# Splitting a float32 product into rounded halves: input halves side by side in one matmul, and expert outputs summed token by feature

## The chip, the cores and the metric

One core of a Trainium2 chip runs the whole program. The time is device time in microseconds from the start to the end of the program, and less is better. The engines are named as in the profile: PE is TensorE (matmuls), PEld its weight loads, DVE VectorE, ACT ScalarE, POOL GpSimd, SP SyncE.

## What is computed

Two blocks on a stream of 256 tokens with 2048 features, in float32. The first block has an RWKV-7 time mix and a sparse attention side by side, then a feed-forward of 16384 experts of which each token picks 8 x 16; the second an HGRN2 layer and a forgetting attention. Cut to the parts that the change touches:

```python
def _rmsnorm(x, g): return x / sqrt(mean(x * x) + eps) * g

xn = _rmsnorm(h, norm_mix_g)
p_rw, q, c_kv, iq, ik, iw, gates = split(xn @ w_in)        # 2048 -> 9320
h = h + (sigmoid(ga) * (y_a @ w_branch_rwkv) + sigmoid(gb) * (y_b @ w_branch_dsa)) @ w_out
hn = _rmsnorm(h, norm_ffn_g)
q = hn @ w_peer_query                                       # keys of the picks
act = gelu(einsum('nd,nhkd->nhk', hn, expert_u[eid]))       # eid: the picked experts
h = h + einsum('nhk,nhkd->nd', gate * act, expert_v[eid])
x = x + hgrn2(norm(x) @ a_w_in) @ a_w_out                   # second block
x = x + forgetting_attention(norm(x) @ b_w_in, k, v, F) @ b_w_out
```

## The kernel before

**Layout.** The stream and nearly all activations lie as [feature, token]: 16 chunks (KD) of 128 partitions by 256 tokens (T). Weights come from memory as tiles of [128, 1024] float32, 512 KB each, on SyncE's queue (`raw`, L348, three slots).

**Float32 by halves.** The matmuls take operands rounded to a shorter float (float32r), so each operand is split exactly into a high and a low part: `half_split` (L354) makes `whi` by a ScalarE copy (L359) and `wlo` by a subtraction on VectorE (L360; for half of the query weights on GpSimd), 512 columns at a time, five slots each. `split` (L396) does the same with activations. A product is then high x high + high x low + low x high.

**Projections.** `proj_steps` (L372) makes one tile of 128 output features: for each of 16 chunks it loads 128 weight columns as the stationary operand and streams 256 tokens, three times (L383 to L385), all into one accumulator `pm` of [128, 256] (two slots, each a bank):

```python
nc.tensor.matmul(ps, hi[:, s], xh, start=(c == 0), stop=False)
nc.tensor.matmul(ps, hi[:, s], xl, start=False, stop=False)
nc.tensor.matmul(ps, lo[:, s], xh, start=False, stop=(c == n - 1))
```

There are 330 such projections of 16 chunks, and 32 of 8 chunks (the two branches' output, `w_br`). `evac` (L594) reads the accumulator on VectorE and multiplies it by the norm's scale R; 274 projections end there, 8 (the attention's queries) in `pair_inputs` (L586), and 48 (`w_out`, `a_w_out`, `b_w_out`) in an addition to the stream.

**Projections with tokens on the partitions.** `tok_steps` (L1331, L1340 to L1342) does it the other way round: 128 tokens of the activations are stationary and 512 weight columns stream, three matmuls for each of two token tiles. The value, key and query blocks of the second block use it.

**Experts.** All 16384 experts are computed densely, in 128 tiles of 128; `ups` (L1094) makes the activations, one projection per tile, up to six groups of 8 tiles ahead. Beside the first of them the queries are scored and the top 16 picked (`select`, L1113: the score matmuls at L1121 read `dq`, what `evac` made of the query projection), then one-hot products make the gate matrix (`onehots`, L1212). `weigh` (L1245) multiplies a group's activations by their gates and splits them (`cs`), and `down` (L1256) sums the group's outputs: for each of 16 feature chunks d, 8 expert tiles x 3 matmuls of 256 columns (L1264 to L1266), then the sum is added to the stream h[d] on VectorE (L1267). 16 groups make 2048 matmuls on each of the three lines.

**Order.** Work is written as generators whose steps `interleave` mixes; the tile scheduler lays out each engine's instructions at compile time by that order and by its own estimate of when each is ready. On the chip every engine runs its list in order. In the HGRN stage `heads` (L1415) is a chain that passes between ACT, DVE, POOL (L1452, L1504) and PE (L1475) while the next projections run beside it.

Of the kernel before, what the change touches and what calls it, by code (L numbers as in the profile page):

```python
# [73 lines left out]
def _consts():  # L74
# [8 lines left out]
    # [128, 16]: column 2j+h of a window that starts at 14-2j is the indicator of half h  # L83
# [20 lines left out]
    # [s, t] inside a tile, t of the second halves of the blocks of 2 * 2**l: pairs that part at level l  # L104
# [4 lines left out]
    # [t, s]: -1e30 above the diagonal  # L109
# [31 lines left out]
def pack(i):  # L141
    """Every input as the kernel loads it: tiles in the order of their use, each contiguous."""
# [98 lines left out]
def interleave(*streams):  # L241
    """(generator, number of its steps): one step of whichever is least far"""
# [16 lines left out]
def after(n, do, steps):  # L259
    """the steps, and do() after n of them"""  # L260
# [5 lines left out]
def lagged(steps, lag):  # L266
    """the generators side by side, each lag steps behind the one before"""
# [13 lines left out]
class Kern:  # L281
    # names of tiles that share slots
    GROUP = {}
    for _g, _n in dict(
        tmp="xc bias sq rs pd th b bx eb ei kk rk st y yo mix relu Rc ck score ld k4",
        mv="rz vz dq",
# [7 lines left out]
    def __init__(self, tc, a, out, es, dbg=None):  # L294
# [7 lines left out]
        self.open("all", ah=17, al=17, nacc=4, nsq=3)  # L302
# [7 lines left out]
    def open(self, name, **slots):  # L310
        """a pool with so many slots for each group of tiles; its memory waits for nothing but the tiles there"""
# [16 lines left out]
    # ---- small helpers  # L328
# [5 lines left out]
    def pm(self, w=T):  # L334
        return self.pp.tile([P, w], F32, name="pm", tag="pm", bufs=2)
# [12 lines left out]
    def raw(self, src):  # L348
        """1024 or 512 columns of weights"""
# [4 lines left out]
    def half_split(self, raw, i, eng=None):  # L354
        """exact (hi, lo) of half i of raw"""
# [12 lines left out]
    def proj(self, src, act, eng=None):  # L368
        """src [128, K]: one tile of 128 output features; act: (hi, lo) of the inputs, per k chunk [128, T]."""
        return finish(self.proj_steps(src, act, eng))  # L370

    def proj_steps(self, src, act, eng=None, ps=None, step=8):  # L372
# [3 lines left out]
        for c in range(n):  # L376
            xh, xl = act[c]
# [18 lines left out]
    def split(self, x, g=None, tag=None, out=None):  # L396
        """exact (hi, lo) of x or x*g, g a column"""
        nc = self.nc
        hi, lo = out or (self.t1(tag or "ah", dt=F32R), self.t1(tag or "al", dt=F32R))
# [6 lines left out]
        return hi, lo  # L406

# [1417 lines left out]
```

## Time and profile before

| | |
|---|---|
| median of 3 runs | 3615.51 us (3613.62 to 3616.02) |
| span of the profiled execution | 3613.2 us |
| TensorE busy | 3563.3 us, 99%, 29630 matmuls |
| VectorE, ScalarE, GpSimd busy | 71%, 52%, 12% |
| memory read | 595 MB, 171 GB/s over the span |

The profiled execution lies 2.3 us below the median of the runs. Busy time of TensorE counts overlapping matmuls as one, so it doesn't tell how close they follow each other; the order in time does. The program's stages by time: mixer to 590 us, branches and output to 870, peer queries to 1110, one-hots to 1340, experts to 2540, HGRN to 3050, forgetting attention to the end.

### The profile page before, as it was taken

The page shows a single profiled execution, that of the slowest core. Times are in us where ns is not written, and L with a number is a line of the kernel's source. Part 1 is how long each engine was busy: PE and PEld are TensorE (multiplying, and loading weights), DVE is VectorE, ACT ScalarE, POOL GpSimd, SP SyncE. Part 2 cuts the span into 40 slices and gives each one's busy share as a digit, 9 for nine tenths or more (in the row PEclk, how much of TensorE's full clock was granted, in tenths as well). Part 3 has the DMA queues.
Part 4 walks back from the last instruction along what each step waited for, and adds up shares of the span by engine and source line. Part 5 has one row for each costly group of instructions (what it writes and reads, how often), then busy time and mean ns, then how long its engine had stood idle before and what let it go on. Part 6 is the DMA issues. An engine that isn't in the chain of part 4 may idle for free.

```text
span 3613.2 us, 76495 instructions
## 1 busy us (share of the span) xinstructions
PE 3563.3 (99%) x29630; PEld 3398.9 (94%) x29630; DVE 2582.2 (71%) x5410; ACT 1874.0 (52%) x3695; POOL 436.8 (12%) x488
## 2 busy tenths in 40 slices
PE   8999999999999999999999999999999999999999
PEld 7888889999999999999999999999899999888899
DVE  6767766666999987666666666667768887657775
ACT  5443444445445664444444444445556665566653
POOL 1121110001234420000000000000013340000010
PEclk9999999999999999999999999999999999999999
DMA  7422225555455677666666665555644436665445
GB/s 224 157 95 77 73 82 158 182 186 194 161 167 176 217 243 245 195 194 195 197 193 195 196 194 184 183 183 181 193 150 139 135 123 185 192 194 169 127 146 179
DMA packets 204636, 619.26 MB, mean 171 GB/s; under 512 B 19520, under 2 KB 60848, under 8 KB 202096
## 3 DMA queue, kind: packets, MB, share of 16 engines
q1 hardware_dynamic: 197616, 604.06, 52.7%
q10 hardware_dynamic: 5888, 8.20, 0.7%
q8 instruction: 234, 3.83, 0.4%
q0 software_dynamic: 768, 2.10, 0.2%
q14 instruction: 130, 1.06, 0.1%
HBM read 595.32 MB, written 21.06 MB: 171 GB/s over the span
## 4 chain that ended last, share of the span: by engine, by line
PE 84%; issue 5%; DVE 5%; DMA 4%; ACT 1%; POOL 1%; SPq 0%; DVEq 0%; ACTq 0%; POOLq 0%
PE pm L383 16%; PE pm L385 15%; PE pm L384 15%; PE pm L1264 6%; PE pm L1266 6%; PE pm L1265 6%; PE pa L758 3%; DVE wlo L360 2%; PE pa L1228 2%; DMA wraw<-w_pq 1%; PE pa L1475 1%; PE pa L1340 1%; PE pa L1341 1%; PE pa L1342 1%; PE pm L1342 1%
## 5 line engine op out<-in xcount | busy, mean ns | idle before, releaser
L360 DVE TENSOR_TENSOR wlo<-wraw,whi 128x512 fp32r<-128x512 f32 x2114 | 1522.3, 725 | 737.4 <-ACT whi L359 690.5
L359 ACT ACTIVATE whi<-wraw 128x512 fp32r<-128x512 f32 x2152 | 1343.9, 631 | 1335.7 <-PE pm L384 706.4
L383 PE MATMUL pm<-ah,whi 128*128 128x256 f32 x4384 | 1279.0, 292 | 1.0 <-ACT nacc L438 1.0
L385 PE MATMUL pm<-ah,wlo 128*128 128x256 f32 x4384 | 1248.4, 285 | 10.4 <-DVE wlo L360 8.5
L384 PE MATMUL pm<-al,whi 128*128 128x256 f32 x4384 | 1245.4, 284 | 0.0
L383 PEld LDWEIGHTS pm<-ah,whi 128*128 128x128 f32 x4384 | 843.5, 192 | 26.0 <-issue 15.7
L385 PEld LDWEIGHTS pm<-ah,wlo 128*128 128x128 f32 x4384 | 843.2, 192 | 16.6 <-DVE wlo L360 12.0
L384 PEld LDWEIGHTS pm<-al,whi 128*128 128x128 f32 x4384 | 844.3, 193 | 0.9
L1264 PE MATMUL pm<-cs,whi 128*128 128x256 f32 x2048 | 581.2, 284 | 1.0 <-ACT whi L359 0.8
L1266 PE MATMUL pm<-cs,wlo 128*128 128x256 f32 x2048 | 580.9, 284 | 0.0
L1265 PE MATMUL pm<-cs,whi 128*128 128x256 f32 x2048 | 580.9, 284 | 0.0
L1264 PEld LDWEIGHTS pm<-cs,whi 128*128 128x128 f32 x2048 | 394.0, 192 | 1.5 <-ACT whi L359 1.5
L1265 PEld LDWEIGHTS pm<-cs,whi 128*128 128x128 f32 x2048 | 394.1, 192 | 0.0
L1266 PEld LDWEIGHTS pm<-cs,wlo 128*128 128x128 f32 x2048 | 394.1, 192 | 0.0
L442 POOL TENSOR_TENSOR nacc<-nacc,nsq 128x256 f32<-128x256 f32 x35 | 29.0, 836 | 1396.6 <-ACT nsq L441 1375.8
L384 PE MATMUL pm<-keep,whi 128*128 128x256 f32 x640 | 181.3, 283 | 0.0
L1267 DVE TENSOR_TENSOR h<-pm,h 128x256 f32<-128x256 f32 x256 | 108.3, 423 | 40.0 <-PE pm L1266 37.1
L384 PEld LDWEIGHTS pm<-keep,whi 128*128 128x128 f32 x640 | 123.2, 193 | 0.0
L1099 ACT ACTIVATE ga<-kk 128x256 f32<-128x256 f32 x128 | 52.9, 413 | 114.4 <-DVE kk L595 114.4
L385 PE MATMUL pm<-keep,wlo 128*128 128x256 f32 x384 | 108.0, 281 | 0.0
L383 PE MATMUL pm<-keep,whi 128*128 128x256 f32 x384 | 108.0, 281 | 0.0
L1340 PE MATMUL pa<-whi,ah 128*128 128x512 f32 x256 | 102.5, 400 | 0.0
(414 smaller groups left out, 5050.5 us busy)
## 6 DMA issues: line engine op xcount, KB each, us to landing
wraw<-peer_u SPq DMA_DIRECT2D x256, 512.0 KB, 3.8
wraw<-peer_v SPq DMA_DIRECT2D x256, 512.0 KB, 3.5
wraw<-w_in SPq DMA_DIRECT2D x136, 512.0 KB, 3.8
wraw<-a_w_in SPq DMA_DIRECT2D x96, 512.0 KB, 3.8
wraw<-w_br SPq DMA_DIRECT2D x32, 512.0 KB, 3.5
wraw<-w_out SPq DMA_DIRECT2D x32, 512.0 KB, 4.3
wraw<-w_pq SPq DMA_DIRECT2D x32, 512.0 KB, 4.3
gates<-gst SPq DMA_DIRECT2D x16, 1024.0 KB, 5.5
```

The lines of the kernel that those rows point to most:

```text
L359: nc.scalar.activation(hi, x, AF.Copy)
L360: (eng or nc.vector).tensor_tensor(lo, x, hi.bitcast(F32), op=OP.subtract)
L383: nc.tensor.matmul(ps, hi[:, s], xh, start=(c == 0), stop=False)
L384: nc.tensor.matmul(ps, hi[:, s], xl, start=False, stop=False)
L385: nc.tensor.matmul(ps, lo[:, s], xh, start=False, stop=(c == n - 1))
L758: nc.tensor.matmul(ps[h, c], lhs[h, c], rhs[h, c], start=True, stop=True)
L1228: nc.tensor.matmul(p[:, v], one[:, v], two[:, v], start=True, stop=True)
L1264: nc.tensor.matmul(ps, hi[:, s], ch, start=(e == 0), stop=False)
L1265: nc.tensor.matmul(ps, hi[:, s], cl, start=False, stop=False)
L1266: nc.tensor.matmul(ps, lo[:, s], ch, start=False, stop=(e == GE - 1))
L1267: nc.vector.tensor_tensor(h[d], ps, h[d], op=OP.add)
L1340: nc.tensor.matmul(ps[tt], xh[:, t], hi, start=(c == 0), stop=False)
```

## The change

**Projections.** The high and low half of an activation now lie side by side in one tile [128, 2, 256] (`pair`), and the accumulator `pm` is 512 columns wide. High weights stream both halves at once, 512 columns; low weights stream the high half, 256 columns, into the first half of the accumulator. At the end the two halves of the accumulator are added: a ScalarE copy of the second half (`pb`, which shares the three slots of `nsq`), then a VectorE addition. The branch projections keep the old form. `evac` multiplies by R on GpSimd afterwards; the three residual additions use `add`, with two VectorE additions.

**Expert outputs.** `down` uses `tok_steps`: the weighted activations are stationary, 512 columns of expert weights stream. Sums stay as [token, feature] in eight SBUF tiles `ys` over all 16 groups and are transposed back and added to h during and after the last group (`back`). The expert weights are laid out anew in memory for it.

**Pools.** Slots are renamed and resized to fit (peer: `keepR`, `tmp` 8 to 7; experts: `cs` 24 to 23, `yt` 8; fox: `keep` 48 to 8 and `keep2` 21 tiles of twice the size).

```diff
-    v = f("peer_v")[0].reshape(P, NG, GE, KD, P)
-    a["peer_v"] = np.ascontiguousarray(v.transpose(1, 3, 0, 2, 4)).reshape(NG, KD, P, GE * P)
+    v = f("peer_v")[0].reshape(P, NG, GE // 2, 2, 4, 512)
+    a["peer_v"] = np.ascontiguousarray(v.transpose(1, 4, 2, 0, 3, 5)).reshape(NG, 4, GE // 2, P, 1024)
...
-    def pm(self, w=T):
+    def pm(self, w=512):
...
     def proj_steps(self, src, act, eng=None, ps=None, step=8):
...
-            xh, xl = act[c]
+            x = act[c]
...
-            nc.tensor.matmul(ps, hi[:, s], xh, start=(c == 0), stop=False)
-            nc.tensor.matmul(ps, hi[:, s], xl, start=False, stop=False)
-            nc.tensor.matmul(ps, lo[:, s], xh, start=False, stop=(c == n - 1))
+            if isinstance(x, tuple):
+                xh, xl = x
+                nc.tensor.matmul(ps[:, :T], hi[:, s], xh, start=(c == 0), stop=False)
+                nc.tensor.matmul(ps[:, :T], hi[:, s], xl, start=False, stop=False)
+                nc.tensor.matmul(ps[:, :T], lo[:, s], xh, start=False, stop=(c == n - 1))
+            elif c < n - 1:
+                nc.tensor.matmul(ps, hi[:, s], x.rearrange("p a t -> p (a t)"), start=(c == 0), stop=False)
+                nc.tensor.matmul(ps[:, :T], lo[:, s], x[:, 0], start=False, stop=False)
+            else:
+                nc.tensor.matmul(ps[:, :T], lo[:, s], x[:, 0], start=False, stop=False)
+                nc.tensor.matmul(ps, hi[:, s], x.rearrange("p a t -> p (a t)"), start=False, stop=True)
...
+    def join(self, ps, out):
+        b = self.t1("pb")
+        self.nc.scalar.activation(b, ps[:, T:], AF.Copy)
+        self.nc.vector.tensor_tensor(out, ps[:, :T], b, op=OP.add)
+
+    def add(self, x, ps, out=None):
+        b = self.t1("pb")
+        self.nc.scalar.activation(b, ps[:, T:], AF.Copy)
+        self.nc.vector.tensor_tensor(x, ps[:, :T], x, op=OP.add)
+        self.nc.vector.tensor_tensor(x if out is None else out, x, b, op=OP.add)
...
+    def pair(self, x, g=None, tag="ah", out=None):
+        t = self.t1(tag, (P, 2, T), F32R) if out is None else out
+        self.split(x, g, out=(t[:, 0], t[:, 1]))
+        return t
...
-        self.nc.vector.scalar_tensor_tensor(q, ps, 0.125, self.R, op0=OP.mult, op1=OP.mult)
+        self.join(ps, q)
+        self.nc.vector.scalar_tensor_tensor(q, q, 0.125, self.R, op0=OP.mult, op1=OP.mult)
...
     def evac(self, ps, out):
-        self.nc.vector.tensor_tensor(out, ps, self.R, op=OP.mult)
+        self.join(ps, out)
+        self.nc.gpsimd.tensor_tensor(out, out, self.R, op=OP.mult)
...
-        self.open("experts", gt=2, cs=24)
+        self.close()
+        self.open("experts", gt=2, cs=23, yt=8)
+        ys = [[self.t1("yt", (P, 512)) for _ in range(4)] for _ in range(2)]
...
+        def back(b):
+            for d in range(4 * b, 4 * b + 4):
+                ps = self.pa(T)
+                s = slice(d % 4 * P, d % 4 * P + P)
+                for tt in range(2):
+                    nc.tensor.transpose(ps[:, tt * P : tt * P + P], ys[tt][b][:, s], self.cst("ident"))
+                yield
+                nc.vector.tensor_tensor(h[d], ps, h[d], op=OP.add)
+                yield
+
         def down(gr, cs):
-            for d in range(KD):
-                w = self.weights(a["peer_v"][gr, d])
-                ps = self.pm()
-                for e, (ch, cl) in enumerate(cs):
-                    if e % 4 == 0:
-                        hi, lo = next(w)
-                    s = slice(e % 4 * P, e % 4 * P + P)
-                    nc.tensor.matmul(ps, hi[:, s], ch, start=(e == 0), stop=False)
-                    nc.tensor.matmul(ps, hi[:, s], cl, start=False, stop=False)
-                    nc.tensor.matmul(ps, lo[:, s], ch, start=False, stop=(e == GE - 1))
-                nc.vector.tensor_tensor(h[d], ps, h[d], op=OP.add)
+            for b in range(4):
+                ps = [self.pa() for _ in range(2)]
+                st = self.tok_steps(a["peer_v"][gr, b], cs, ps)
+                if gr == NG - 1 and b:
+                    interleave((st, 16), (seq((None,) * 2, back(b - 1)), 16))
+                else:
+                    finish(st)
+                for tt in range(2):
+                    if gr:
+                        nc.vector.tensor_tensor(ys[tt][b], ps[tt], ys[tt][b], op=OP.add)
+                    else:
+                        nc.scalar.activation(ys[tt][b], ps[tt], AF.Copy)
...
+        finish(back(3))
...
-            ttv(self.x[c], ps, self.x[c], op=OP.add)
+            self.add(self.x[c], ps)
...
-        self.open("fox", keep=48, tmp=12, V=1, c2=1, yt=4, rows=4, mask=1, pl=3)
+        self.open("fox", keep=8, keep2=21, tmp=12, V=1, c2=1, yt=4, rows=4, mask=1, pl=3)
...
-            ttv(o, ps, x[c], op=OP.add)
+            self.add(x[c], ps, o)
```

## Rows read from the trace of the kernel before

**Rows 1.** the page: span, then busy time of each engine

```profile
span 3613.2 us, 76495 instructions
PE 3563.3 (99%) x29630; PEld 3398.9 (94%) x29630; DVE 2582.2 (71%) x5410; ACT 1874.0 (52%) x3695; POOL 436.8 (12%) x488
```

**Rows 2.** expert outputs in time: start us, us, instruction; 24 matmuls apart

```profile
2000.09 0.28 PE L1265 MATMUL pm<-cs,whi 128*128 128x256 f32 x1
...
2002.97 0.28 PE L1265 MATMUL pm<-cs,whi 128*128 128x256 f32 x1
```

**Rows 3.** the same, 512 columns, fox blocks; 12 matmuls apart

```profile
3249.73 0.39 PE L1342 MATMUL pa<-whi,al 128*128 128x512 f32 x1
...
3252.45 0.39 PE L1342 MATMUL pa<-whi,al 128*128 128x512 f32 x1
```

**Rows 4.** L384 by stretch: us, PE (x), PEld (x), clock, DMA, GB/s

```profile
0.00:590.00 590.00, 241.65 (x847) 163.31 (x848) 1.00 0.37 117
590.00:900.00 310.00, 241.74 (x850) 164.15 (x850) 0.99 0.60 190
900.00:1340.00 440.00, 280.80 (x991) 190.53 (x991) 1.00 0.58 191
1340.00:2650.00 1310.00, 379.07 (x1336) 257.33 (x1336) 1.00 0.62 195
2650.00:2960.00 310.00, 178.18 (x627) 121.42 (x626) 0.99 0.41 132
2960.00:3613.20 653.20, 250.37 (x888) 169.96 (x887) 1.00 0.55 169
```

**Rows 5.** stretches, all engines: us, PE, PEld, DVE, ACT, POOL, clock, DMA, GB/s

```profile
900.00:1340.00 440.00, 428.45 (x3557) 423.34 (x3557) 406.26 (x896) 232.29 (x388) 155.25 (x114) 1.00 0.58 191
1340.00:2650.00 1310.00, 1308.89 (x10546) 1292.74 (x10546) 873.89 (x1574) 658.75 (x1173) 10.93 (x14) 1.00 0.62 195
2650.00:2960.00 310.00, 297.15 (x2464) 293.92 (x2463) 262.12 (x534) 195.28 (x400) 108.66 (x124) 0.99 0.41 132
```

**Rows 6.** the page's groups: names, shapes, count, busy us, mean ns, idle before

```profile
L1264 PE MATMUL pm<-cs,whi 128*128 128x256 f32 x2048 | 581.2, 284 | 1.0 <-ACT whi L359 0.8
```

**Rows 7.** transposes in time, fox blocks: start us, us, instruction, four merged

```profile
3222.92 0.60 PE L1607 MATMUL pa<-consts,yt 128*128 128x128 f32 x4
```

**Rows 8.** groups of DVE and POOL from 1140 to 1300 us, in the one-hots

```profile
L360 DVE TENSOR_TENSOR wlo<-wraw,whi 128x512 fp32r<-128x512 f32 x81 | 79.1, 995 | 0.0
L1234 DVE TENSOR_TENSOR oh<-consts,keep 128x512 f32<-128x512 f32 x53 | 52.0, 982 | 0.0
L1235 DVE TENSOR_TENSOR oh<-consts,keep 128x512 f32<-128x512 f32 x53 | 36.0, 678 | 0.0
L1231 POOL TENSOR_TENSOR oh<-oh,keep 128x512 f32<-128x512 f32 x53 | 68.8, 1298 | 91.9 <-DVE oh L1235 78.0 <-PE pm L385 6.3 <-PE pm L384 5.7
```

**Rows 9.** groups of DVE from 1700 to 2200 us, POOL idle

```profile
L360 DVE TENSOR_TENSOR wlo<-wraw,whi 128x512 fp32r<-128x512 f32 x347 | 239.7, 692 | 155.9 <-ACT whi L359 147.3
L1267 DVE TENSOR_TENSOR h<-pm,h 128x256 f32<-128x256 f32 x87 | 36.9, 424 | 15.1 <-PE pm L1266 13.3
```

**Rows 10.** groups of POOL and DVE from 2650 to 2960 us, HGRN heads

```profile
L1504 POOL TENSOR_TENSOR t<-t 128x256 f32<-128x256 f32 x52 | 42.6, 819 | 71.8 <-ACT t L1458 65.1 <-PE pm L384 3.3 <-PE pm L385 2.5
L1508 DVE TENSOR_TENSOR Ad<-pa,consts 128x512 f32<-128x512 f32 x7 | 4.7, 678 | 0.0
```

**Rows 11.** groups of ACT: a copy of 256 columns out of PSUM

```profile
L1124 ACT ACTIVATE score<-pa 128x256 f32<-128x256 f32 x16 | 6.0, 375 | 5.7 <-PE pa L1121 5.7
```

**Rows 12.** evacuations (L595) by stretch: us, DVE busy (x), clock, DMA, GB/s

```profile
900.00:1340.00 440.00, 25.43 (x62) 1.00 0.58 191
2650.00:2960.00 310.00, 16.41 (x39) 0.99 0.41 132
```

**Rows 13.** line L1121: its engine sat idle until: us, times

```profile
  DVE dq L595: 10.3, 16
```

**Rows 14.** line L1475: its engine sat idle until: us, times

```profile
  DVE t L1466: 11.5, 11
```

More of the change, by code (lines that the diff above doesn't have):

```diff
@@ L483, in mixer @@
         src = [a["w_in"][0], a["w_in"][1], a["w_misc"][0], a["w_in"][10], a["w_in"][11]]
[L484 removed]
+        lead = [self.proj_steps(w, self.xn, ps=self.pa(), step=4) for w in src]
         for c in range(KD + 4):
             if c < KD:
[L487 removed]
+                self.xn.append(self.pair(xs[c], self.par("g_mix", c)))
                 self.sq_acc(acc, xs[c])
@@ L1080, in peer @@
         h = self.h
-        self.open("peer", mv=3, keep=12, tmp=8, ga=LEAD * GE + 4)
+        self.open("peer", keepR=1, tmp=7, ga=LEAD * GE + 4)
+        self.open("select", mv=3, keep=12)
         acc = {}
@@ L1084, in peer @@
         for c in range(KD):
-            hn.append(self.split(h[c], self.par("g_ffn", c)))
+            hn.append(self.pair(h[c], self.par("g_ffn", c)))
             self.sq_acc(acc, h[c])
         def scale():
-            self.R = yield from self.rms_steps(self.mean_sq(acc))
+            self.R = yield from self.rms_steps(self.mean_sq(acc), tag="keepR")
         ga = []
@@ L1277, in peer @@
                 finish(ups(GE))
-        for c in range(KD):
-            self.tap(f"p{c}", h[c])
+        finish(back(3))
         self.close()
@@ L1295, in final_norm @@
         for c in range(KD):
-            xa.append(self.split(h[c], gw[:, c : c + 1]))
+            xa.append(self.pair(h[c], gw[:, c : c + 1]))
             self.sq_acc(acc, h[c])
@@ L1333, in tok_steps @@
         nc = self.nc
-        for c2 in range(KD // 2):
+        n = 2 * src.shape[0]
+        for c2 in range(n // 2):
             for k, (hi, lo) in enumerate(self.weights(src[c2])):
                 c = 2 * c2 + k
-                xh, xl = act[c]
+                xh, xl = act[c] if isinstance(act[c], tuple) else (act[c][:, 0], act[c][:, 1])
                 for tt in range(2):
@@ L1540, in gates @@
                 sg.append(self.silu2(g))
-        pair = []
         def new(hd):
-            if hd % 2 == 0:
-                pair[:] = [self.t1("keep2" if hd < 8 else "t2", (P, 2, T), F32R) for _ in range(2)]
-            return [t[:, hd % 2] for t in pair]
+            return self.t1("keep2" if hd < 8 else "t2", (P, 2, T), F32R)
         ya = []
@@ L1617, in gated @@
             nc.gpsimd.tensor_tensor(y, oh[hd], sg[hd], op=OP.mult)
-            res.append(self.split(y, out=new(hd)))
+            res.append(self.pair(y, out=new(hd)))
             yield
@@ L1629, in fox @@
         for c in range(KD):
-            xk.append(self.split(x[c], self.par("kv_nw", c)))
+            xk.append(self.pair(x[c], self.par("kv_nw", c)))
             self.sq_acc(acc, x[c])
@@ L1689, in split_again @@
             for c in range(KD):
-                xb.append(self.split(x[c], self.par("b_nw", c)))
+                xb.append(self.pair(x[c], self.par("b_nw", c)))
                 yield
@@ L1709, in norm @@
                 t = [slice(u * P, u * P + P) for u in range(4)]
-                out = [self.t1("keep") for _ in range(4)]
+                out = [t[:, i] for t in [self.t1("keep2", (P, 2, T)) for _ in range(2)] for i in range(2)]
                 res.extend(out)
@@ L1720, in heads, with half @@
             return lambda ps: (seq(norm(ps), then()), 26)
+        pairs = {}
+        def half(name, hd):
+            if hd % 2 == 0:
+                pairs[name] = self.t1("keep2", (P, 2, T))
+            return pairs[name][:, hd % 2]
         def attention(heads):
@@ L1764, in attend @@
             nc.tensor.matmul(po[:, P:T], pt[:, T:], V[:, 1, hv], start=False, stop=True)
-            o = self.t1("keep")
+            o = half("o", hd)
             oh.append(o)
@@ L1776, in gates @@
             for hd in heads:
-                gt = self.t1("keep")
+                gt = half("g", hd)
                 self.evac((yield from self.proj_steps(a["b_w_g"][hd], xb)), gt)
@@ L1781, in fox @@
         y = []
-        out = self.gated(oh, sg, lambda hd: [self.t1("keep", dt=F32R) for _ in range(2)], y)
+        out = self.gated(oh, sg, lambda hd: self.t1("keep2", (P, 2, T), F32R), y)
         at = lambda *h: lambda: attention(range(*h))
```

22 lines of the change are left out of this document (11 added, 11 removed).

## The prediction

> **What bounds the kernel now.** I read the page first, then the instruction groups of TensorE, the order of its matmuls in time, and the same stretches of the program seen from every engine. The page says TensorE is busy for 3563 of 3613 us and VectorE for 71% [rows 1]. A busy TensorE doesn't yet mean a TensorE that can go no faster, since matmuls overlap, so the view that matters is the start-to-start distance. In the expert stage 24 distances between matmuls of 256 columns take 2.88 us, that is 120.0 ns each [rows 2]. Where the moving side is 512 columns, 12 distances take 2.72 us, that is 226.7 ns [rows 3]. The granted clock is 1.00 (2.4 GHz) in the stretches that hold both [rows 4], so the columns alone take 106.7 and 213.3 ns: either width pays 13.3 ns more, once per matmul. Two matmuls of 256 cost 240 ns and one of 512 costs 227 ns. TensorE takes its work at these distances nearly everywhere; in the stretch from 1340 to 2650 us VectorE is busy 67% and ScalarE 50% of the time, and TensorE does not wait for them [rows 5]. The exceptions are 900 to 1340 us (peer queries and one-hots: VectorE 406 of 440 us) and 2650 to 2960 us (HGRN heads: VectorE 262 of 310 us, in a chain that hops between four engines) [rows 5]. There I have to ask whether TensorE's gain can be used.
>
> **The change part by part.**
>
> *Projections.* A chunk of 128 inputs was three matmuls of 256 columns, 3 x 120.0 = 360.0 ns. It becomes one of 512 and one of 256: 226.7 + 120.0 = 346.7 ns, 13.3 ns less, with the same number of columns. Counting the middle matmul (L384) by stretch gives 847, 850, 991, 1336, 627 and 888 chunks [rows 4]; 256 of the 850 belong to the branch projections (32 projections of 8 chunks), which keep three matmuls. By stretch the gain is 11.3, 7.9, 13.2, 17.8, 8.4 and 11.8 us; together 5280 chunks (330 projections of 16; the few more in the rows are counted on both sides of an edge), 70.4 us. No row of before shows widths by turns. Below, each matmul's distance holds its own columns and one weight load in either order, and I see no reason for more; the other end is that no gain is made, which is a rival.
>
> *Expert outputs.* There are 3 x 2048 matmuls of 256 columns [rows 6]. They become 3072 of 512 in exactly the pattern of rows 3: 6144 x 120.0 = 737.3 us against 3072 x 226.7 = 696.4 us, 40.9 us less. Added are 32 transposes of 128 x 128 to bring the sum back. Four in a row span 0.60 us [rows 7]; a matmul is shown some 0.16 us longer than the distance to its next (0.28 against 0.12, 0.39 against 0.23) [rows 2, 3], so (0.60 - 0.16) / 4, about 0.11 us each: 3.5 us. They run between the matmuls of the last group, only the last 8 after it. Of those the next stage needs features in order and takes 16 us (12 chunks x 6 x 226.7 ns) to reach them; I put 1 us on this seam (0 to 4). VectorE adds 128 blocks of 512 columns at about 0.68 us [rows 10] instead of 256 of 256 columns at 0.42 us [rows 9]: 87 us for 109 us, in a stage where it idles a third of the time. Loads keep their number and size on SyncE's queue; the consumers take them 4 to 6% faster.
>
> *Getting the halves together.* Each of the 330 projections adds a ScalarE copy of 256 columns out of PSUM, 0.38 us [rows 11], in all 124 us on an engine that has half its time free; it is charged nothing for throughput. VectorE's one pass stays one, an add of PSUM and SBUF; 48 residual adds and 8 query evacuations get a second one of 0.42 us, 24 us in all, hidden but for the very last, which lengthens the tail by 0.4 us. The two slots of a projection's sum are reused one projection later; copy and add are done 0.6 us after it ends, a projection takes 16 x 346.7 ns = 5.5 us, so no slot is waited for. 274 projections are also scaled, now by GpSimd on two SBUF tensors. A GpSimd operation of this shape takes 0.82 us [rows 10]. That is the costly edit. In most stretches GpSimd is idle and nobody needs the result soon (activations run six groups ahead): nothing.
>
> It is not nothing where VectorE is full. The low-half split of the weights (L360) takes 692 ns on VectorE while GpSimd is idle [rows 9], and 995 ns from 1140 to 1300 us, where GpSimd is busy 69 of 160 us [rows 8]. These 81 splits lost 24.5 us and their sisters at L1234 (982 ns against 678 for the same shape at L1235, 53 of them) 16 us: 40 us per 69 us of GpSimd, 0.6 us of VectorE for each microsecond of GpSimd. The Trainium skill (SBUF — State Buffer, Who interferes with whom) goes further: a VectorE instruction with two SBUF inputs and a GpSimd one that reads SBUF exclude each other for a whole instruction. By that rule the price would be 1.0 instead of 0.6; the trace agrees on the effect and shows the smaller price.
>
> The stretch 900 to 1340 us has 62 evacuations [rows 12], 51 us more of GpSimd, so 31 us of VectorE at 0.6. VectorE had 34 us free, but TensorE wants the stretch 13.2 us shorter: the gain doesn't fit, and the stage stays at about 440 us. Besides, the 16 query results now pass ScalarE, VectorE and GpSimd before the score matmuls (L1121) which TensorE waits for in order. It waited 10.3 us for them [rows 13]. The path grows by 0.38 + 0.82 us and two hand-overs, some 1.5 us, times 16 is 24 us; part is covered by the projection steps that are put in between, and GpSimd may be busy with an earlier split. I take 6 us (0 to 24). The stretch 2650 to 2960 us has 39 evacuations [rows 12], 32 us of GpSimd on top of 109, 19 us of VectorE, which has 48 free; but TensorE waits there for a link of the chain (11.5 us at L1475 [rows 14]) in which GpSimd has two links per level. I let it keep its length: the 8.4 us are lost, no more. Of the first 590 us I take 8.3 of the 11.3 us, as its early evacuations feed the next steps at once.
>
> *Sum.* 70.4 + 40.9 = 111.3 us; less 21.6 (gain of both dense stretches), 6 (query results), 3 (opening), 3.5 (transposes), 1 (seam), 0.4 (tail) leaves 75.8 us. The profiled span is 3613.2 us, so 3537.4 us; the median of the runs, 3615.5, lies 2.3 us above the span, which I keep: **3540 us**. Its own range is 3518 to 3562.
>
> **The rivals.**
>
> *The dense stretches gain too.* For it: TensorE still runs at 97% from 900 to 1340 us [rows 5], and GpSimd's multiply may fall on moments when VectorE reads PSUM. Then 111.3 - 3.5 - 1.4 = 106 us are kept: 3509 us. Against it: VectorE's 92% there.
>
> *The multiply is dearer.* At 1.0 us of VectorE per microsecond of GpSimd, 62 evacuations cost 51 us where 34 are free, and the 24 us of query waits come whole: dense stretches 17 + 24 + some 10 in the HGRN chain over their old length, 45 us above the forecast's 6: 3585 us. **On the other side, slower than before**, lies the same mechanism at its worst: 101 multiplies of the dense stretches, each delaying TensorE by its full 0.82 us (83 us), and the 16 query results each behind two GpSimd operations of some 1.4 us (45 us). That is 128 us against the 82 us which the rest of the sum gains, 3661 us. It decides from 0.8 us of lost TensorE time per dense evacuation. Against it: VectorE's 34 and 48 free microseconds would have to be useless.
>
> *Widths by turns don't save.* If a chunk still takes 360 ns, because a 512 after a 256 pays the fee twice, only the 40.9 us remain: 3615.5 - 40.9 + 4.9 + 6, about 3586 us. For it: no row has the pattern. Against it: the extra 256 columns cost 106.7 ns, their bare time, in rows 2 and 3, so the fee belongs to the matmul and not to the columns. The Trainium skill (TensorE: Matmul & The Clock Gate, Back-to-back issue gap) gives a fee of 2.5 ns per matmul in place of 13.3; by that, 8352 fewer matmuls are worth 21 us and the time would be near 3606 us. The trace shows 13.3 ns.
>
> **How the numbers follow.** Forecast 62% (3518 to 3562), dense stretches gain too 22% (3500 to 3518), multiply dearer 11% (3562 to 3610, of it 3% beyond, slower than before), no saving by turns 5% (3575 to 3600). For 8 in 10 the range goes from 3505 to 3575. A measurement can tell 0.2% (7 us) from nothing: faster by more 95%, same 2%, slower 3%.
>
> **What would show it.** In the expert stage a matmul of 512 columns every 227 ns and in projections 227 and 120 by turns; if a pair takes 360, the third rival holds. The stretch up to the end of the one-hots should be about 440 us long with VectorE near 95%; shorter by 13 us is the first rival, longer by 20 the second. The idle time before the score matmuls should rise from 10 us to 15 to 35 us. The splits on VectorE should be slower only there. I am wrong altogether if the order laid out by the scheduler puts a ScalarE copy that waits for a projection's end ahead of a split which TensorE needs; then new waits of TensorE on whi would stand in stages that had none.

## The result: slower, where a gain of 2% was forecast

The changed kernel takes 3632.86 us (median of four runs, 3629.37 to 3635.84) against 3614.57 us of the kernel before: a ratio of 1.0054, 95% interval 1.004 to 1.0069. The forecast was 3540 us, with a range of 3505 to 3575. One run of those further below, of 8127.67 us with the query results scaled on VectorE, fell into the slow state and is left out. The page of the profiled execution, span and busy times (answering to [rows 1]):

```profile
span 3633.8 us, 59848 instructions
PE 3518.8 (97%) x21310; PEld 2957.8 (81%) x21310; DVE 2639.3 (73%) x5346; ACT 1951.5 (54%) x4033; POOL 716.9 (20%) x762
```

TensorE has 8320 matmuls fewer and is busy for 45 us less, and still the span is 21 us longer: TensorE now idles for 115 us instead of 50. GpSimd has 280 us more.

**The distances.** TensorE in order of time after the change; start us, us, instruction. First the projections of the expert stage, seven chunks:

```profile
1901.01 0.40 PE L392 MATMUL pm<-ah,whi 128*128 128x512 f32 x1
1901.25 0.28 PE L393 MATMUL pm<-ah,wlo 128*128 128x256 f32 x1
1901.36 0.40 PE L392 MATMUL pm<-ah,whi 128*128 128x512 f32 x1
...
1903.48 0.40 PE L392 MATMUL pm<-ah,whi 128*128 128x512 f32 x1
```

From 1901.01 to 1903.48 seven chunks take 2.47 us, 353 ns each, not 346.7. Then the expert outputs, six matmuls apart (answering to [rows 2, 3]):

```profile
2100.79 0.39 PE L1389 MATMUL pa<-wlo,cs 128*128 128x512 f32 x1
...
2102.15 0.39 PE L1389 MATMUL pa<-wlo,cs 128*128 128x512 f32 x1
```

That is 1.36 us for six, 227 ns each, as forecast.

**The stretches.** All engines by stretch (columns as in [rows 5]). Of before, the queries (first to last score matmul) and the one-hots (first to last one-hot matmul), which the prediction had read as one stretch, and the HGRN stage:

```profile
909.80:1094.00 184.20, 177.90 (x1443) 173.64 (x1444) 168.34 (x540) 81.51 (x146) 60.42 (x42) 1.00 0.50 163
1123.90:1319.40 195.50, 195.50 (x1670) 195.50 (x1670) 189.19 (x246) 120.80 (x187) 79.47 (x61) 1.00 0.64 216
2546.60:2995.10 448.50, 435.50 (x3260) 416.68 (x3259) 362.58 (x720) 269.02 (x533) 125.42 (x143) 0.99 0.47 148
```

The same three after the change:

```profile
911.00:1116.40 205.40, 179.83 (x981) 153.41 (x982) 173.93 (x539) 90.58 (x176) 85.44 (x72) 0.96 0.45 148
1146.10:1356.90 210.80, 199.35 (x1285) 174.44 (x1284) 198.22 (x247) 124.30 (x211) 104.86 (x87) 1.00 0.58 197
2537.20:3005.50 468.30, 439.09 (x2544) 382.53 (x2543) 384.88 (x731) 282.32 (x586) 170.92 (x185) 0.98 0.43 141
```

The queries grew by 21 us, the one-hots by 15 and HGRN by 20. In the queries TensorE is busy about as long as before (177.9 and 179.8 us); what is added is waiting. What the score matmuls waited for (answering to [rows 13]: us, times), and the link of the HGRN chain ([rows 14]):

```profile
  POOL dq L627: 54.3, 30
```

```profile
  DVE t L1514: 30.2, 14
```

In the queries 10.3 us became 54.3, and the releaser is now GpSimd. Both counts hold a weight load and its matmul; the matmuls alone waited 4.4 us before and 24.8 us after. In HGRN 11.5 us became 30.2, but the matmuls alone went from 9.3 to 14.0 us only: the rest are weight loads, whose waits before stand under "issue" (9.0 us). In the one-hots it is groups and waits that tell (columns as in [rows 8]; the last line is a wait: us, times, longest):

```profile
L1267 DVE TENSOR_TENSOR oh<-consts,keep 128x512 f32<-128x512 f32 x61 | 66.1, 1084 | 0.0
```

```profile
ACT ga L1132 <- POOL kk L627: 89.0, 25, 5.1
```

VectorE's one-hot comparison with two SBUF inputs takes 1084 ns (961 in the same stage of before), and ScalarE's activations stand waiting for what GpSimd makes of `kk`, with the weight copies `whi` behind them in ScalarE's order. Of these 89.0 us only some 20 are new: in the kernel without the multiply, below, they wait 68.6 us there for VectorE's `kk`. TensorE's matmuls wait 6.7 us for `wlo` and 4.3 us for `whi` in this stage. The multiply itself (the page's group):

```profile
L627 POOL TENSOR_TENSOR kk<-kk,keepR 128x256 f32<-128x256 f32 x128 | 145.2, 1134 | 865.6 <-DVE kk L404 865.6
```

On `kk` it takes 1134 ns in the mean, where the forecast had 0.82 us.

### The profile page after: what moved, and what is told of

It is laid out like the page before. It is cut to its first block, busy times and chain, and to the rows that moved or that the text cites. A ratio compares the mean times of both kernels' runs of the same rounds, so it can differ in the third digit from the quotient of the medians.

```text
span 3633.8 us, 59848 instructions
## 1 busy us (share of the span) xinstructions
PE 3518.8 (97%) x21310; PEld 2957.8 (81%) x21310; DVE 2639.3 (73%) x5346; ACT 1951.5 (54%) x4033; POOL 716.9 (20%) x762
## 4 chain that ended last, share of the span: by engine, by line
PE 59%; DVE 7%; ACT 3%; POOL 3%; issue 2%; DMA 1%; ACTq 0%; POOLq 0%; DVEq 0%
PE pm L392 17%; PE pm L393 9%; PE pa L1388 8%; PE pa L1389 8%; PE pa L1390 8%; DVE wlo L362 2%; PE pm L1390 1%; PE pm L1389 1%; PE pm L1388 1%; PE pa L1261 1%; PE pm L396 1%; PE pa L1523 1%; ACT whi L361 1%; DMA wraw<-w_pq 1%; PE pm L395 1%
## 5 line engine op out<-in xcount | busy, mean ns | idle before, releaser
L392 PE MATMUL pm<-ah,whi 128*128 128x512 f32 x4110 | 1517.8, 407 | 5.1 <-ACT whi L361 4.3
L393 PE MATMUL pm<-ah,wlo 128*128 128x256 f32 x4110 | 1167.0, 284 | 21.4 <-DVE wlo L362 19.0
L392 PEld LDWEIGHTS pm<-ah,whi 128*128 128x128 f32 x4110 | 779.7, 190 | 190.0 <-issue 15.9
L1388 PE MATMUL pa<-whi,cs 128*128 128x512 f32 x1024 | 399.5, 390 | 0.0
L1390 PE MATMUL pa<-whi,cs 128*128 128x512 f32 x1024 | 398.5, 389 | 0.0
L1389 PE MATMUL pa<-wlo,cs 128*128 128x512 f32 x1024 | 398.4, 389 | 0.0
L627 POOL TENSOR_TENSOR kk<-kk,keepR 128x256 f32<-128x256 f32 x128 | 145.2, 1134 | 865.6 <-DVE kk L404 865.6
L1390 PEld LDWEIGHTS pa<-whi,cs 128*128 128x128 f32 x1024 | 192.2, 188 | 40.2
L1389 PEld LDWEIGHTS pa<-wlo,cs 128*128 128x128 f32 x1024 | 192.3, 188 | 39.5
L1388 PEld LDWEIGHTS pa<-whi,cs 128*128 128x128 f32 x1024 | 192.3, 188 | 39.2
L403 ACT ACTIVATE pb<-pm 128x256 f32<-128x256 f32 x274 | 105.5, 385 | 185.2 <-PE pm L396 184.8
L392 PE MATMUL pm<-keep,whi 128*128 128x512 f32 x368 | 132.1, 398 | 1.1 <-DVE keep L426 1.0
L396 PE MATMUL pm<-ah,whi 128*128 128x512 f32 x274 | 110.6, 404 | 0.0
L1388 PE MATMUL pm<-whi,ah 128*128 128x512 f32 x256 | 101.9, 398 | 0.0
```

Source lines behind the costliest of these rows:

```text
L392: nc.tensor.matmul(ps, hi[:, s], x.rearrange("p a t -> p (a t)"), start=(c == 0), stop=False)
L393: nc.tensor.matmul(ps[:, :T], lo[:, s], x[:, 0], start=False, stop=False)
L396: nc.tensor.matmul(ps, hi[:, s], x.rearrange("p a t -> p (a t)"), start=False, stop=True)
L403: self.nc.scalar.activation(b, ps[:, T:], AF.Copy)
L627: self.nc.gpsimd.tensor_tensor(out, out, self.R, op=OP.mult)
L1388: nc.tensor.matmul(ps[tt], xh[:, t], hi, start=(c == 0), stop=False)
```

## The experiments

Theory after the result: the scaling on GpSimd costs what was lost, by holding back VectorE and by being late for those who read it. Rivals: 512 and 256 columns by turns don't save what was forecast, or the new expert sums don't. Each ratio below is to runs of the kernel before that were made beside it (medians of 3610 to 3615 us), so a few microseconds of a difference between two of these kernels can be that.

**One half of the change at a time.** Narrow projections with the new expert sums:

```diff
+WIDE = False
...
-            if isinstance(x, tuple):
-                xh, xl = x
+            if isinstance(x, tuple) or not wide:
+                xh, xl = x if isinstance(x, tuple) else (x[:, 0], x[:, 1])
...
     def evac(self, ps, out):
+        if not self.is_wide[id(ps)]:
+            self.nc.vector.tensor_tensor(out, ps[:, :T], self.R, op=OP.mult)
+            return
```

> The changed kernel with its projections put back to three matmuls of 256 columns and the old evacuation; the new expert sums stay. Theory (the expert part brings its gain, the projections lose it again): 6144 matmuls at 120 ns become 3072 at 227 ns, 41 us less, 3.5 us for the transposes and about 1 us at the seam: 3578 us (3570 to 3588), queries and one-hots as long as before. Rival (the expert part itself costs something, at the seam or by the larger loads of its sums): above 3600 us.

Measured: 3571.97 us, ratio 0.9884 [0.9867, 0.99]. Wide projections with the old expert sums (`down` and the layout of `peer_v` as before):

> The changed kernel with the old expert sums (16 feature chunks of 24 matmuls of 256 columns); the wide projections stay. Theory: the changed kernel less the expert gain of 37 us, so 3633 + 37 = 3670 us (3660 to 3680): the projections alone make the kernel some 55 us slower, in the queries, one-hots and HGRN heads. Rival (the two parts disturb each other, so that either alone is good): below 3620 us.

Measured: 3661.72 us, ratio 1.0133 [1.0116, 1.015]. The expert sums bring about 42 us beside narrow projections and 29 beside wide ones; the wide projections lose 47 us beside the old sums and 61 beside the new ones. The two halves are not independent, and where the 13 us between them go is open, but the rival that the expert sums gain nothing falls.

**The scaling, moved and left out.** On VectorE instead of GpSimd:

```diff
-        self.nc.gpsimd.tensor_tensor(out, out, self.R, op=OP.mult)
+        self.nc.vector.tensor_tensor(out, out, self.R, op=OP.mult)
```

> The changed kernel with the multiplication by R on VectorE instead of GpSimd, 274 more VectorE operations of 0.42 us. If what costs is GpSimd (its 1.13 us per operation and its lock on VectorE's second input), this is faster than the changed kernel: 0.42 us of VectorE for 1.13 us of GpSimd: 3600 us (3590 to 3615). If what costs is VectorE's load alone, it is the same or slower: 3630 to 3645 us, since 62 and 39 operations are 26 and 16 us more of VectorE in the dense stretches.

Measured: 3607.55 us, ratio 0.9987 [0.9977, 0.9996]. Then without that line:

> The changed kernel without the multiplication by the norm's scale on GpSimd in the 274 evacuations: the scaling by R is left out, everything else is the same. Theory (GpSimd's multiplication, through its lock on VectorE and the wait behind it, makes the dense stretches longer): queries 21, one-hots 15 and HGRN heads 20 us shorter than in the changed kernel, less what the added copy and hop still cost: 3580 us (3570 to 3595). Rival (the longer path through ScalarE and VectorE and the two extra hand-overs do it, whatever the third step): 3615 us or more.

Measured: 3546.51 us, ratio 0.981 [0.9794, 0.9827]; 3570 to 3595 was expected, so the multiply costs more than the growth of the three stages. The multiply on GpSimd costs 86 us; as a second pass on VectorE it costs 61.

**Work or wait?** The GpSimd multiply stays, but writes into the tile of the second half (`pb`, which `join` now returns), and nobody reads that any more:

```diff
-        self.join(ps, out)
-        self.nc.gpsimd.tensor_tensor(out, out, self.R, op=OP.mult)
+        b = self.join(ps, out)
+        self.nc.gpsimd.tensor_tensor(b, out, self.R, op=OP.mult)
```

> The changed kernel in which GpSimd does its 274 multiplications by R as before but into the tile of the second half, which nobody reads; the consumers take the unscaled sum, so the scaling is left out of the result. If GpSimd's work beside VectorE is the price (the lock on the second input), nearly all of the 85 us between the changed kernel and the one without the multiplication stays: 3615 us (3600 to 3630). If the price is the wait for the multiplication on the way to the score matmuls and in the HGRN chain, the time falls to that of the kernel without it: 3550 us (3545 to 3565). I expect a division: the one-hots stay at 211 us (lock), the queries fall from 205 to about 192 us, the HGRN heads from 387 to about 370 us; 3580 us.

Measured: 3612.03 us, ratio 1.0005 [0.9995, 1.0014]: 65 of the 86 us are there although nobody reads the result, where about 34 of them had been expected (3580 us). Quite without waits it isn't: what overwrites the tile that the multiply reads must wait for it (ScalarE 33.5 us before the gates' activations, VectorE 8.7 us), but none of this is in the queries, the one-hots or the experts. The counter-test puts the same unread multiply into the narrow kernel of the first run, whose evacuations are as before:

```diff
             self.nc.vector.tensor_tensor(out, ps[:, :T], self.R, op=OP.mult)
+            self.nc.gpsimd.tensor_tensor(self.t1("pb"), out, self.R, op=OP.mult)
```

> The kernel with the expert sums alone (narrow projections, scaled on VectorE as before the change), plus one GpSimd multiplication of 256 columns after each of its 266 evacuations that go through the common helper, into a tile nobody reads. It prices GpSimd's work by itself, with no longer path and no wider matmul. If the lock is the price: one-hots from 195 to about 207 us, queries from 187 to about 195 us, HGRN heads from 368 to about 380 us, the whole 3572 + 32 = 3604 us (3590 to 3620). If only the longer path costs: 3574 us (3570 to 3580).

Measured: 3637.9 us, ratio 1.0068 [1.0051, 1.0085], 66 us more than without, twice the 32 expected (the trace counts 274 multiplies). The control has a ScalarE copy of the same 256 columns in its place:

```diff
+            self.nc.scalar.activation(self.t1("pb"), out, AF.Copy)
```

> The kernel of the narrow projections with the new expert sums, and after each of the 274 evacuations a ScalarE copy of the 256 columns, in the place of the GpSimd multiply of the run before; nobody reads its result. Nothing of the computation is left out. It is the control for that run, in which 274 unread GpSimd multiplies cost 66 us. If that was GpSimd's presence beside VectorE (or its own queue), the same instruction on ScalarE, which is busy about half of the time, costs little: 3572 to 3585 us. If it was the added instruction as such, by a changed order of the other engines' work or by the wait for the evacuation, the time is again near 3638 us.

Measured: 3583.3 us, ratio 0.992 [0.9897, 0.9943], 11 us more than without. So it is not that an instruction was added, but that GpSimd has it. The pages' busy times: narrow, narrow with the unread GpSimd multiply, narrow with the unread ScalarE copy.

```profile
PE 3518.7 (99%) x26590; PEld 3231.2 (91%) x26590; DVE 2552.6 (72%) x5290; ACT 1877.8 (53%) x3703; POOL 435.4 (12%) x488
```

```profile
PE 3553.6 (98%) x26590; PEld 3258.8 (90%) x26590; DVE 2643.8 (73%) x5290; ACT 1879.9 (52%) x3703; POOL 719.6 (20%) x762
```

```profile
PE 3523.3 (98%) x26590; PEld 3235.7 (90%) x26590; DVE 2547.4 (71%) x5290; ACT 1960.2 (55%) x3977; POOL 439.7 (12%) x488
```

With GpSimd busy 284 us longer the same 5290 VectorE instructions take 91 us more; with ScalarE busy 82 us longer they take no more. A part of the 66 us can be TensorE's clock: the mean granted clock is 0.998 in the narrow kernel, 0.997 with the copy and 0.992 with the multiply, and 0.006 of 3640 us is 22 us, an upper bound of that part. Where this lands, by the stages' lengths in us, each from the first and last uses in its trace (the last line is the span less the others, so it holds the gaps on either side of the one-hots as well as what follows HGRN):

| stage | before | after | no multiply | multiply unread | narrow | narrow, unread multiply |
|---|---|---|---|---|---|---|
| opening, to the end of RWKV | 576.1 | 579.6 | 569.1 | 582.0 | 573.9 | 583.9 |
| branches, to the first score | 333.7 | 331.4 | 329.6 | 331.2 | 331.9 | 333.2 |
| queries | 184.3 | 205.4 | 187.9 | 191.2 | 186.9 | 190.3 |
| one-hots | 195.5 | 210.8 | 192.1 | 205.0 | 195.5 | 204.3 |
| experts | 1199.9 | 1152.3 | 1153.7 | 1152.1 | 1163.7 | 1162.5 |
| HGRN, to the first `a_w_out` | 448.5 | 468.3 | 439.3 | 465.9 | 449.0 | 475.6 |
| the rest | 675.2 | 686.0 | 676.6 | 688.5 | 668.6 | 690.6 |

In the experts the multiply costs nothing, read or not; unread it costs 12.9 of 18.7 us in the one-hots and 26.6 of 29.0 in HGRN; in the queries only the one that is read costs much. The one-hots without it, and with it unread (all engines), and then for how long TensorE's weight loads and matmuls waited for VectorE's splits in the one and in the other (us, times, longest):

```profile
1116.50:1308.70 192.20, 192.20 (x1285) 174.61 (x1284) 188.68 (x246) 124.62 (x212) 78.59 (x61) 1.00 0.64 217
```

```profile
1135.00:1340.00 205.00, 196.06 (x1285) 174.73 (x1284) 202.81 (x246) 123.63 (x211) 107.44 (x87) 1.00 0.58 202
```

```profile
PEld pm L393 <- DVE wlo L362: 1.0, 4, 0.3
```

```profile
PEld pm L393 <- DVE wlo L362: 13.2, 14, 1.2
PE pm L393 <- DVE wlo L362: 8.4, 13, 0.8
```

28.9 us more of GpSimd lengthen the same VectorE instructions by 14.1 us (splits 985 to 1035 ns, comparisons 961 to 1112 ns), TensorE's matmuls wait 8.4 us for VectorE's splits, and the stage is 12.8 us longer. HGRN in the same two kernels:

```profile
2489.50:2928.70 439.20, 429.60 (x2540) 375.11 (x2539) 362.91 (x731) 281.73 (x585) 130.57 (x145) 1.00 0.46 150
```

```profile
2521.70:2987.60 465.90, 438.70 (x2538) 381.81 (x2537) 381.56 (x731) 281.51 (x585) 168.35 (x185) 0.98 0.41 142
```

VectorE grows from 362.9 to 381.6 us, the stage by 26.6. But there GpSimd also has links of the chain, and the unread multiply stands before one of them in GpSimd's order. GpSimd in time, then what ScalarE waited for the second of these links, without the multiply and with it unread:

```profile
2721.44 1.29 POOL L1484 TENSOR_TENSOR t<-t,t 128x512 f32<-128x512 f32 x1
2727.52 1.71 POOL L628 TENSOR_TENSOR pb<-t,keep 128x256 f32<-128x256 f32 x1 [4.79 <-DVE t L404]
2729.19 1.30 POOL L1485 TENSOR_TENSOR t<-t,t 128x512 f32<-128x512 f32 x1
```

```profile
ACT t L1505 <- POOL t L1483: 1.2, 2, 0.7
```

```profile
ACT t L1507 <- POOL t L1485: 19.5, 7, 4.0
```

GpSimd stood still for 4.8 us until VectorE had added the halves of a projection, and only then did the multiply and the link behind it. These waits grew by 18.3 us. TensorE, besides, is busy 9.1 us longer for the same matmuls, at a granted clock of 0.98 instead of 1.00. How the 26.6 us divide between the queue, VectorE's slowing and the clock wasn't told apart.

**The queries' wait by itself.** Only the 16 query results are scaled on VectorE, the rest on GpSimd:

```diff
-    def evac(self, ps, out):
+    def evac(self, ps, out, eng=None):
         self.join(ps, out)
-        self.nc.gpsimd.tensor_tensor(out, out, self.R, op=OP.mult)
+        (eng or self.nc.gpsimd).tensor_tensor(out, out, self.R, op=OP.mult)
...
-            self.evac(ps, q)
+            self.evac(ps, q, nc.vector)
```

> The changed kernel with the 16 query results alone scaled on VectorE; the other 258 stay on GpSimd. The score matmuls waited 54 us for these 16 in the changed kernel, 10 us before. If that wait is what makes the query stretch 21 us longer, it falls from 205 us to about 192 us and the whole to 3620 us (3612 to 3626). If VectorE's lock by the other multiplications does it, the stretch stays at 203 us or more and the whole at 3631 us (3626 to 3638).

Measured: 3650.07 us (median of three), ratio 1.0104 [1.0084, 1.0124]: slower still. The waits from the first to the last score matmul (engine, line, releaser: us, times, longest), of the changed kernel and of this one:

```profile
PEld pa L1154 <- POOL dq L627: 29.6, 15, 3.9
PE pa L1154 <- POOL dq L627: 24.8, 15, 3.6
PE pm L393 <- DVE wlo L362: 2.8, 2, 2.5
```

```profile
PEld pm L393 <- DVE wlo L362: 31.2, 21, 2.5
PE pm L393 <- DVE wlo L362: 21.2, 21, 2.2
PEld pa L1154 <- DVE dq L627: 17.3, 15, 1.8
PE pa L1154 <- DVE dq L627: 12.6, 15, 1.4
ACT whi L361 <- DMA wraw<-w_pq: 26.6, 12, 2.8
ACT whi L361 <- DMA wraw<-peer_u: 25.7, 12, 3.1
```

The wait for the query results fell, and the projections began to wait for VectorE's splits instead; the stage took 220.6 us, where about 192 or 203 and more had been expected. VectorE is not busier for it (173.7 us, 173.9 in the changed kernel). Its splits wait 25.0 us for ScalarE's copies, and these 52.3 us for weights from memory (18.8 in the changed kernel). So the 15 us are not VectorE's busy time; an order of the work that brings the weights later is as likely, and the cause is open. All that is shown is that neither place tried for this operation is cheap in this stage.

**The distances of the projections.** In each group of four chunks, four matmuls of 512 and then four of 256:

```diff
-            elif c < n - 1:
-                nc.tensor.matmul(ps, hi[:, s], x.rearrange("p a t -> p (a t)"), start=(c == 0), stop=False)
-                nc.tensor.matmul(ps[:, :T], lo[:, s], x[:, 0], start=False, stop=False)
...
+                if c < n - 1:
+                    wide_mm()
+                if c % 4 == 3:
+                    for b in range(4):
+                        sb = slice(b * P, b * P + P)
+                        nc.tensor.matmul(ps[:, :T], lo[:, sb], act[c - 3 + b][:, 0], start=False, stop=False)
+                if c == n - 1:
+                    wide_mm()
```

> The changed kernel with the two widths sorted inside each group of 4 chunks: four matmuls of 512, then the four of 256 (in a projection's last group the 256s before the last 512). In the changed kernel a chunk takes 353 ns at TensorE, not 346.7. Theory A (changing from one width to the other costs the missing 6.4 ns): the group takes 4 x 346.7 plus at most one toll, some 5 ns less per chunk; 5280 chunks make 25 us where TensorE sets the pace, about 18 us of it outside the dense stretches: 3615 us (3605 to 3622). Theory B (the toll belongs to each matmul of 512 with weights as the stationary side): chunk still 353 ns, 3633 us (3626 to 3640).

Measured: 3623.53 us, ratio 1.0022 [1.0013, 1.0032], 9 us better than by turns and between the two theories. TensorE in time, equal neighbours merged:

```profile
2000.96 1.09 PE L392 MATMUL pm<-ah,whi 128*128 128x512 f32 x4
2001.89 0.63 PE L400 MATMUL pm<-ah,wlo 128*128 128x256 f32 x4
2002.36 0.86 PE L392 MATMUL pm<-ah,whi 128*128 128x512 f32 x3
2003.06 0.63 PE L400 MATMUL pm<-ah,wlo 128*128 128x256 f32 x4
```

Four chunks take 1.40 us, 350 ns each: four matmuls of 512 in 0.93 us and three in 0.70, 233 ns each, and four of 256 in 0.47 us, 118 each. With the low-weight matmuls left out altogether, only 512 after 512 remain:

```diff
...
-                nc.tensor.matmul(ps[:, :T], lo[:, s], x[:, 0], start=False, stop=False)
...
```

> The changed kernel with the matmuls of the low weights left out of the wide projections, so that only matmuls of 512 columns follow each other there (that part of the product is missing). If changing widths costs the extra time, their distance is 227 ns as in the token blocks; if it belongs to this arrangement (weights stationary, both halves streaming), it is 233 to 236 ns. Looked at in the expert stage alone; the whole time, some 3100 us, says nothing.

```profile
1699.21 2.43 PE L392 MATMUL pm<-ah,whi 128*128 128x512 f32 x10
```

Ten of them, less the 0.39 us that one is shown to last, over nine distances: 227 ns. (The time of that run, 3298 us, says nothing, as a third of the columns of these products is missing.) So neither these operands nor the wider accumulator are slow by themselves. That the change of width is what costs is not shown, though: over the expert stage of the grouped run two neighbours of 512 columns are 234 ns apart (median of 950), without any change between them, against 227 (1270) with the low weights left out. By turns it is 236 ns from a 512 to the next 256 and 117 from a 256 to the next 512. What makes a 512 slower in a projection that has 256s as well is open.

**Wide only where VectorE or GpSimd has room.** RWKV up to `w_out` (scaled on VectorE), experts (GpSimd) and forgetting gates (VectorE) wide; the rest narrow as before, with queries, one-hots and HGRN in it:

```diff
-            if isinstance(x, tuple):
-                xh, xl = x
+            if isinstance(x, tuple) or not wide:
+                xh, xl = x if isinstance(x, tuple) else (x[:, 0], x[:, 1])
...
-        self.nc.gpsimd.tensor_tensor(out, out, self.R, op=OP.mult)
+        self.scaler.tensor_tensor(out, out, self.R, op=OP.mult)
...
+        self.wide, self.scaler = True, nc.gpsimd
         for gr in range(NG):
...
+        self.wide, self.scaler = False, nc.vector
```

> The new expert sums everywhere; wide projections only in the RWKV part and the output projections of the mixer (scale on VectorE), in the expert stage (scale on GpSimd, which is idle there) and in the gates of the forgetting attention (scale on VectorE); three matmuls of 256 in the opening, the queries, the one-hots, the HGRN layer and the last output projection. Theory (the stages add up): 3572 us of the experts alone, less 5 (RWKV), 6 (branches and output), 11 (experts) and 2 (gates): 3548 us (3540 to 3556). Rival (wide projections don't pay anywhere for themselves): 3570 us or more.

Measured: 3555.76 us, ratio 0.9836 [0.982, 0.9853]. With the grouping on top:

> The kernel with wide projections only where the other engines have slack, and in these the widths sorted in groups of 4 chunks. With 3.5 ns less per chunk (1400 ns in place of 4 x 353 for a group) in the expert stage (84 projections), the mixer's later part and the gates, together some 170 projections of 16 chunks, about 9 us less where TensorE sets the pace: 3548 us (3543 to 3555). If the coarser order of its steps costs as much elsewhere, 3556 us as before the sorting.

Measured: 3551.0 us, ratio 0.9828 [0.9812, 0.9844]: the best version, 61 us below the runs of before beside it (3612.16 us).

## Why the prediction was wrong, by its own steps

**The expert sums: right.** 40.9 us less 3.5 and 1 were forecast, 36.4. Beside narrow projections the experts' stage became 36.2 us shorter (1199.9 to 1163.7), and the whole 3614 - 3572, about 42 us; the other 6 lie in the rest, with no cause shown. The added transposes and additions cost no more than put down.

**The distance of a pair: a term of the wrong size.** The step "each matmul's distance holds its own columns and one weight load in either order, and I see no reason for more" failed for the projections. A pair costs 353 ns, not 346.7; of the 13.3 ns per chunk 7 are left. At 5280 chunks 6.3 ns are 33 us. The stages agree: the experts gained 1163.7 - 1152.3 = 11.4 us by wide projections, where 17.8 were forecast. This is half of the third rival, which I had given 5%. Its size came by half; its reason, that a 512 after a 256 pays the fee twice, did not, since in the grouped run a 512 after a 512 is nearly as slow. The Trainium skill (TensorE: Matmul & The Clock Gate, Back-to-back issue gap) has a fee of 2.5 ns per matmul, in the gap of single matmuls; a pair here pays 353 - 320 = 33 ns, and no run shows so small a fee.

**The multiply: the right mechanism at less than half its price.** Charged were 21.6 us for the dense stretches, 6 for the queries and 3 for the opening, 31 in all. Without the multiply the kernel is 86 us faster, so 55 us were missing. It wasn't the price in VectorE time: 14.1 us for 28.9 us of GpSimd in the one-hots is 0.5, and I took 0.6. The step that failed is "VectorE had 34 us free", from which the stage "stays at about 440 us", and with it the "48 free" of HGRN. The 34 us are true of 900 to 1340 us as a whole, but by stage VectorE had 6.3 us free of 195.5 in the one-hots and 15.9 of 184.2 in the queries; the rest lay in the gaps between. In the one-hots there was no room for 14 us: the stage lost 18.7 us, 12.9 of them with the result unread. In the queries room was not the matter (the unread multiply cost 3.3 us) but the wait, see below. The two stages together lost 36 us, where 13.2 and 6 had been put down. For HGRN the 48 us of VectorE left out GpSimd's order: the multiply stands before a link of the chain and waits there for a projection's sum. In that stage it cost 29 us (468.3 against 439.3), where 8.4 had been given up. The opening cost 10.5 us instead of 3, the rest 9.4 instead of nothing; unread the multiply costs as much in both (12.9 and 11.9), and why is open.

The Trainium skill (SBUF — State Buffer, Who interferes with whom) has a VectorE instruction with two SBUF inputs and a GpSimd one that reads SBUF shut each other out for a whole instruction. The runs agree on the effect; the price they show is not one for one: 91 us of VectorE for 284 us of GpSimd over the narrow kernel.

**The query results: mis-sized.** Charged were 6 us out of a range of 0 to 24. The stage lost 17.5 us against the kernel without the multiply, and 14.2 of it is gone once nobody reads the result. The sign named was a wait that rises from 10 to between 15 and 35 us; 54.3 us came by the same count, which has loads and matmuls both. Of the matmuls alone, for which TensorE stands still, it is 4.4 us and 24.8. So the path was as long as the upper end had it, and what was wrong is the 6, by which the projection steps put in between would have covered most of it. The granted clock of this stretch is 0.96 where it was 1.00. Time at 1.2 GHz, the lower level, stands behind waits of up to 3.9 us here; 4 in 100 below full speed over 205 us is 8 us, an upper bound of what the clock gave away, and part of the same loss.

**The second rival and its point.** "The multiply is dearer" is what happened, and it turned the sign. I had let it decide from 0.8 us of lost TensorE time per evacuation in the dense stretches. Measured are (17.5 + 18.7 + 29.0) / 101 = 0.65 us, below that point: it needed the 33 us lost at the pairs as well. Two errors of the same direction, held to be independent small risks (11% and 5%), add up: 55 + 33 = 88 of the 93 us. The 5 us left are a balance. Without the multiply the wide projections gain 25.5 us beside the new sums (3571.97 - 3546.51), where 7 ns on 5280 chunks would be 37; the expert sums brought 6 more than forecast. After HGRN the kernel without the multiply takes 6 us longer than the narrow one (619.6 against 613.4), and there lie 32 of the 48 residual additions with two passes; that these are the cause was only argued.

**Signs named beforehand.** 227 and 120 by turns: no, 353 the pair. The stretch to the end of the one-hots longer by 20, the second rival's sign: yes, by 36 (about 21 and 15). Splits slower only there: no. In the one-hots they are as before (986 ns against 985) and the comparisons slower (1084 against 961); they are slower in the queries (868 against 813), but in the opening (750 against 720) and the branches (752 against 712) too. The new waits on `whi` named last stayed small, 4.3 us in front of the 4110 matmuls of L392 that read `ah`.

## What to carry to other kernels

An operation moved to an idle engine is free only if the engine beside it does not slow down and nothing urgent stands behind it in the idle engine's order. Before giving GpSimd work on SBUF, look at how full VectorE is stage by stage, not over a stretch of two stages, and at what GpSimd has to do next; then test with the same work unread. A price per instruction read from a row of one size holds for that row; if the change mixes sizes, measure the mix. Make such a change only in the stages that have room for it: here that gave 3556 us, and 3551 with the grouping, against 3572 with narrow projections throughout and 3633 with wide ones throughout.

## What the runs showed of the hardware that I had not expected

Matmuls of 512 and 256 columns run at 227 and 120 ns among their own kind, and at 353 ns for a pair by turns (6.3 ns over the sum); grouped by four, 350 ns per pair. With a quarter of the changes of width half of the extra time stayed, and inside a group the 512s are still 234 ns apart, so the change of width does not account for it. Its cause is open.

GpSimd work whose result nobody reads costs time by itself, beside VectorE and by its place in GpSimd's order: 274 multiplies of 256 columns cost 66 us, 0.24 us each in the mean, none of it in the expert stage where VectorE has a third of its time free, and 25 of them 9 us in the one-hots. A ScalarE copy of the same tiles cost 11 us.
